# Seven block products in the down projections of a two-half-step SwiGLU layer, with the sums of x kept in DRAM

## The chip, the cores and the metric

The kernel runs on one core of a Trainium2 chip. The metric is the device time of one execution in microseconds (us), lower is better. TensorE (PE) multiplies, VectorE (DVE) and ScalarE (ACT) do elementwise work, GpSimd (POOL) issues accumulating DMAs and small things, SyncE (SP) issues the loads of the weights.

## The reference

One decoder layer on x of 256 rows and 2048 columns, all in float32:

```python
x = x + 0.5 * swiglu(rms_norm(x, ffn1_norm), ffn1_w_gate, ffn1_w_up, ffn1_w_down)
x = x + hybrid_mixer(rms_norm(x, mix_norm), ...)       # attention and gated linear attention
x = x + cross_attention(rms_norm(x, xattn_norm), rms_norm(mem, mem_norm), ...)
x = x + 0.5 * swiglu(rms_norm(x, ffn2_norm), ffn2_w_gate, ffn2_w_up, ffn2_w_down)

def swiglu(h, w_gate, w_up, w_down):
    return (jax.nn.silu(h @ w_gate) * (h @ w_up)) @ w_down
```

The hidden width D_FF is 5632. The change touches only the two SwiGLU half steps (`ffn1` and `ffn2`).

## The kernel before

**Precision.** Each float32 operand is a sum of two parts, high and low: ACT casts the high part (`wh`), DVE subtracts it to get the low part (`wl`). A product is three matmuls: high times high, high times low, low times high. `split` does this for a weight group of four K tiles by 512 columns (128 x 2048 elements, 1 MB); `wh` and `wl` have three buffers. The raw weights have six buffers in the half steps, loaded ahead by SP in the order of the program.

**A half step** (`ffn`). The hidden width is cut into 11 blocks of 512 columns, in three parts, `PARTS = ((0,1,2,3),(4,5,6,7),(8,9,10))`. For each block f of a part, gate and up are computed (K = 2048: four groups of K), then silu and the product, and `turn` transposes the result into `hT[f]`. At the end of a part the down projection adds the part's share to x: for each of four output chunks c of 512 columns, `proj` runs over the part's blocks (three or four groups of K), and the result goes into `xs[c]` on DVE. After the last part each finished chunk gets `after(c)`: the norm of the next stage (squares on ACT, transposes on PE), or in the second half step the store.

**Seven products.** For blocks 1 to 10, gate and up are computed as a pair: for the first two groups of K, the two row blocks of x (128 rows each), the two groups and the two matrices make a 2 x 2 by 2 x 2 block product, computed with seven products instead of eight (`head` and its inner `rest`). A product is 12 matmuls of 128 x 512. It needs sums of weight groups, made on DVE (`add`) and by accumulating DMAs on POOL (`accumulate`), and four sums of blocks of x, high and low (`sums`), made once in a half step by `sums_of` and kept in SBUF for the whole half step. `head` runs the first two products, whose results go to PSUM (`x`, `y`) and from there by ACT into `c0l` (`acc`) and `ys`; `rest` runs the others, subtracts on DVE (`c0r`, `c1r`), and then runs the plain groups (`mm3`, 24 matmuls a group). `ahead` calls the next pair's `head` before the last plain group. Block 0 is computed plainly, since the sums aren't there yet; while it runs, `load_x` brings x in, and ACT takes its squares for the norm r, which the activation needs.

**Order.** A scheduler orders the instructions of each engine by priority (`tc.high_priority`) and its own estimate of times; on the chip each engine works in that order.

Of the kernel before, what the change touches and what calls it, by code (L numbers as in the profile page):

```python
# [16 lines left out]
P = 128  # L17
# [30 lines left out]
def layer_kernel(ctx: ExitStack, tc: tile.TileContext, A: dict, out: bass.AP):  # L48
# [10 lines left out]


    phase = {}

    def open_phase(name, half_step):
        phase.update(half_step=half_step, loads=0,
# [8 lines left out]
    def FT(tag, bufs, shape, dt, name):  # L73
        return phase["pool"].tile(shape, dt, tag=tag, name=name, bufs=bufs)
# [61 lines left out]
    def split(wh, wl, src):  # L136
        SC.copy(wh, src)  # L137
        last_split[:] = [V.tensor_sub(wl, src, wh.bitcast(F32)).ins]  # L138
# [33 lines left out]

    def sums_of(ga, gb, put):
# [11 lines left out]
        for i, x in enumerate((sa, sb)):  # L187
            split(*put(i), x)

    def product(acc, lhs, w, start):  # L190

# [13 lines left out]
    def head(Wl, cl, Wr, cr, lhs, ab, sums):  # L205
# [5 lines left out]
        def parts(src):  # L211
            with tc.high_priority(WPRI):
                wh, wl = split_tiles(4, 512)
                split(wh, wl, src)
            return wh, wl
# [10 lines left out]
            return lambda k: lhs(4 * g + k, t)  # L226

        def s_(i):
            return lambda k: tuple(x[:, i, k] for x in sums)

        x, y = PM([P, 512], "x"), PM([P, 512], "y")
        c0l = pa.tile([P, 512], F32, tag="acc", name="acc")
# [7 lines left out]
            ys = W2([P, 512], "ys")  # L240
            SC.copy(ys, y)

        def rest(groups, ahead=None):
            c0r, c1r = (pa.tile([P, 512], F32, tag="acc", name="acc") for _ in range(2))
            add(ral, ral, rbr)
            product(x, s_(1), parts(ral), False)
            with tc.high_priority(WPRI):
                V.tensor_sub(c0r, ys, x)
            product(c0l, of(b, 0), parts(rbl), False)
            accumulate(ral, rbl)  # L250
            product(x, s_(2), parts(rar), False)
            with tc.high_priority(WPRI):
                V.tensor_sub(c1r, ys, x)
# [103 lines left out]
    def ffn(pre, r, after, fine=None, last=False):  # L357
# [14 lines left out]
            sl = slice(t * P, (t + 1) * P)  # L372
            return tuple(p[:, k % 4, sl] for p in hT[k // 4])

        sums = None
        heads = {}

        def begin(f):
            heads[f] = head(wg, f, wu, f, lhs_x, (0, 1), sums)

        for part in PARTS:
            for f in part:
                ahead = (lambda f=f: begin(f + 1)) if f + 1 in part else None
                if sums is None:
                    gate = proj(wg, f, lhs_x, range(4), fine)
                    if callable(r):
                        r = r()
                else:
                    gate, upv = heads.pop(f)((2, 3), ahead)
                sg = []  # L390
                with tc.high_priority(WPRI):
                    for t in range(TT):
                        s = W2([P, 512], "sg")
                        SC.activation(s, gate[t], AF.Silu, scale=r[:, t:t + 1])
                        sg.append(s)
                if sums is None:
                    sums = tuple(FT(n, 1, [P, 4, 4, P], F32R, n) for n in ("sh", "sl"))
                    with tc.issue_after(last_split[0]):
                        sums_of(xT[0], xT[1], lambda i: tuple(p[:, 2 * i:2 * i + 2] for p in sums))
                    upv = proj(wu, f, lhs_x, range(4), ahead=ahead)  # L400
                hs = []
                with tc.high_priority(WPRI):
# [3 lines left out]
                        hs.append(h)  # L406
                later(2, lambda f=f, hs=hs: turn(f, hs))
            end = part is PARTS[-1]
            for c in range(NC):
                ahead = (lambda: begin(part[-1] + 1)) if c == NC - 1 and not end else None  # L410
                acc = proj(wd, c, lhs_h, part, last=last and end and c == NC - 1, ahead=ahead)
                for t in range(TT):
                    V.scalar_tensor_tensor(xs[c][:, t], acc[t], 0.5, xs[c][:, t], op0=ALU.mult, op1=ALU.add)  # L413
                if end:
                    after(c)


    def head_scale(acc, r, r2, t, scale_in, sign, name):
# [627 lines left out]
```

## Time and profile before

| | |
|---|---|
| median of 3 runs | 1932.91 us (1932.5 to 1933.68) |
| profiled execution, its own time | 1933.82 us |
| its span | 1932.0 us |
| PE, DVE, ACT, POOL busy | 99%, 65%, 51%, 5% |
| HBM read | 370.72 MB |
| granted TensorE clock, mean | 0.997 |

The page of the profile gives the busy time of each engine, the chain of work that ended last, and groups of instructions by line, with the tile written, an arrow and the tiles read. Timeline rows give start, duration, engine, line, operation and, in brackets, how long the engine sat idle before and what released it. Rows by windows give, for a stretch, the busy time and number of instructions of each engine, the granted clock (PEclk, 1.00 is full), the busy share of the 16 DMA engines and their GB/s. Line 138 is the subtraction and line 137 the cast of a split, 165 to 167 the three matmuls of a plain group, 196 a product's matmul, 219 a sum of weights on DVE, 223 one by DMA, 235 and 241 the copies to `c0l` and `ys`, 248 and 253 the subtractions out of PSUM, 289 the low part of `hT`, 315 the squares, 394 the silu, 413 the addition into x, 468 the loads of x.

### The profile page before, as it was taken

What the parts mean: (1) busy time and instruction counts of PE and PEld (TensorE: products, weight loads), DVE (VectorE), ACT (ScalarE), POOL (GpSimd) and SP (SyncE); (2) the same over time, 40 slices, a digit from 0 to 9 for tenths busy, and PEclk for the clock granted to TensorE, in tenths of its full rate; (3) what the DMA queues carried; (4) which work ended last, traced back from release to release, by engine and by line L of the source; (5) the groups of instructions that cost most, each with busy time, mean ns of one, the idle gap of its engine ahead of it and who ended that gap; (6) DMA issues with size and microseconds to landing.
All of it is one profiled execution on the core that took longest, in us unless ns stands there. A gap on an engine that the chain in (4) does not pass through costs nothing.

```text
span 1932.0 us, 21279 instructions
## 1 busy us (share of the span) xinstructions
PE 1916.0 (99%) x8760; PEld 1589.1 (82%) x8760; DVE 1265.0 (65%) x956; ACT 981.6 (51%) x881; POOL 90.3 (5%) x95
## 2 busy tenths in 40 slices
PE   8999999999999999999999999999999999999999
PEld 6888888888888888778888889888888888888887
DVE  6786567774678555445776554878656777467853
ACT  6555345553456446444566445655534555445542
POOL 0000000000000000012221000000000000000000
PEclk8999999999999999999999999999999999999999
DMA  9677568775577634445456554577755777557861
GB/s 370 224 234 264 194 189 278 254 258 196 167 247 271 233 124 157 168 155 189 174 209 226 179 191 153 222 241 234 263 195 186 272 264 258 193 166 251 267 245 54
DMA packets 63293, 416.14 MB, mean 215 GB/s; under 512 B 7099, under 2 KB 8251, under 8 KB 14428
## 3 DMA queue, kind: packets, MB, share of 16 engines
q1 hardware_dynamic: 55996, 370.22, 51.2%
q0 software_dynamic: 5760, 41.95, 10.5%
q10 hardware_dynamic: 1440, 2.62, 0.4%
q8 instruction: 68, 1.11, 0.2%
q14 instruction: 29, 0.24, 0.0%
HBM read 370.72 MB, written 2.10 MB: 193 GB/s over the span
## 4 chain that ended last, share of the span: by engine, by line
PE 96%; DMA 1%; DVE 1%; ACT 1%; POOL 0%; issue 0%; SPq 0%; ACTq 0%; POOLq 0%
PE acc L166 22%; PE acc L167 22%; PE acc L165 22%; PE x L196 11%; PE acc L196 6%; PE y L196 3%; PE x L167 2%; PE x L165 2%; PE x L166 2%; DMA raw<-in_ffn_w_gate_dram 1%; PE tp L366 1%; DVE wl L138 0%; PE tp L326 0%; ACT wh L137 0%; POOL gsr L686 0%
## 5 line engine op out<-in xcount | busy, mean ns | idle before, releaser
L138 DVE TENSOR_TENSOR wl<-raw,wh 128x2048 fp32r<-128x2048 f32 (+2 forms) x410 | 920.4, 2259 | 537.8 <-ACT wh L137 536.4
L137 ACT CAST wh<-raw 128x2048 fp32r<-128x2048 f32 (+2 forms) x410 | 769.8, 1889 | 767.3 <-PE acc L167 467.0
L165 PE MATMUL acc<-wh,xTh 128*128 128x512 f32 x1024 | 402.5, 394 | 5.0 <-ACT wh L137 5.0
L166 PE MATMUL acc<-wl,xTh 128*128 128x512 f32 x1024 | 400.7, 391 | 3.6 <-DVE wl L138 3.6
L167 PE MATMUL acc<-wh,xTl 128*128 128x512 f32 x1024 | 400.4, 391 | 0.0
L165 PE MATMUL acc<-wh,hTh 128*128 128x512 f32 x704 | 274.7, 390 | 0.0
L167 PE MATMUL acc<-wh,hTl 128*128 128x512 f32 x704 | 274.0, 389 | 0.0
L166 PE MATMUL acc<-wl,hTh 128*128 128x512 f32 x704 | 273.9, 389 | 0.0
L165 PEld LDWEIGHTS acc<-wh,xTh 128*128 128x128 f32 x1024 | 192.6, 188 | 46.7 <-ACT wh L137 6.3
L166 PEld LDWEIGHTS acc<-wl,xTh 128*128 128x128 f32 x1024 | 193.4, 189 | 45.1 <-DVE wl L138 5.4
L167 PEld LDWEIGHTS acc<-wh,xTl 128*128 128x128 f32 x1024 | 193.2, 189 | 40.6
L167 PEld LDWEIGHTS acc<-wh,hTl 128*128 128x128 f32 x704 | 132.1, 188 | 27.4
L166 PEld LDWEIGHTS acc<-wl,hTh 128*128 128x128 f32 x704 | 132.2, 188 | 27.2
L165 PEld LDWEIGHTS acc<-wh,hTh 128*128 128x128 f32 x704 | 132.2, 188 | 27.2
L219 DVE TENSOR_TENSOR raw<-raw 128x2048 f32<-128x2048 f32 x40 | 91.7, 2292 | 1.4
L223 POOL DMA_DIRECT2D raw<-raw x40 | 34.7, 867 | 1142.5 <-DVE raw L219 939.3
L165 PE MATMUL x<-wh,xTh 128*128 128x512 f32 x160 | 62.2, 389 | 0.0
L166 PE MATMUL x<-wl,xTh 128*128 128x512 f32 x160 | 62.2, 389 | 0.0
L167 PE MATMUL x<-wh,xTl 128*128 128x512 f32 x160 | 62.2, 389 | 0.0
L413 DVE SCALAR_TENSOR_TENSOR x<-acc,x 128x512 f32<-128x512 f32 x48 | 33.0, 688 | 27.2 <-PE acc L167 27.2
L165 PE MATMUL acc<-wh,mTh 128*128 128x512 f32 x128 | 50.1, 392 | 0.0
L167 PE MATMUL acc<-wh,mTl 128*128 128x512 f32 x128 | 49.8, 389 | 0.0
(301 smaller groups left out, 1916.4 us busy)
## 6 DMA issues: line engine op xcount, KB each, us to landing
raw<-in_ffn_w_up_dram SPq DMA_DIRECT2D x88, 1024.0 KB, 6.7
raw<-in_ffn_w_down_dram SPq DMA_DIRECT2D x88, 1024.0 KB, 4.8
raw<-in_ffn_w_gate_dram SPq DMA_DIRECT2D x85, 1024.0 KB, 4.8
raw<-in_w_in_dram SPq DMA_DIRECT2D x48, 1024.0 KB, 4.8
raw<-raw POOLq DMA_DIRECT2D x40, 1024.0 KB, 7.1
raw<-in_w_out_dram SPq DMA_DIRECT2D x16, 1024.0 KB, 4.8
raw<-in_xattn_w_k_dram SPq DMA_DIRECT2D x4, 1024.0 KB, 4.8
raw<-in_xattn_w_q_dram SPq DMA_DIRECT2D x4, 1024.0 KB, 4.8
```

What stands on the lines that cost most here:

```text
L137: SC.copy(wh, src)
L138: last_split[:] = [V.tensor_sub(wl, src, wh.bitcast(F32)).ins]
L165: PE.matmul(acc[t], lh, wh, start=first and i == 0, stop=False, skip_group_check=seeded)
L166: PE.matmul(acc[t], lh, wl, start=False, stop=False, skip_group_check=seeded)
L167: PE.matmul(acc[t], ll, wh, start=False, stop=last and i == len(half) - 1, skip_group_check=seeded)
L196: PE.matmul(acc, lhs(k)[i], w[:, k], start=first, stop=j == 1 and k == 3, skip_group_check=not start)
L219: V.tensor_add(dst, x, y)
L223: G.dma_start(dst, x, accum_op=ALU.add)
L366: PE.transpose(tp[:, j], hs[t][:, j * P:(j + 1) * P], ident)
L413: V.scalar_tensor_tensor(xs[c][:, t], acc[t], 0.5, xs[c][:, t], op0=ALU.mult, op1=ALU.add)
```

## The change

The down projections use the seven products too: chunks are taken in pairs (0, 1) and (2, 3), as the left and right matrix of `head`, with the first two blocks of the part as the two groups of K. The other blocks of the part (two, or one in the last part) run as plain groups. This needs sums of blocks of `hT`, which `sums_of_halves` makes once a part, after the last product of the part's last block that uses sums of x (`mid`). The tiles of the sums are now four of one tag `s`, shared by x and h: the sums of x are written to DRAM once in a half step (`first_sums`), by DMAs of POOL, and are loaded back at the start of the second and third part (`load_sums`). In the last group of the second half step, `last` keeps the order of one row block after the other. The loads of x get lower priorities, one lower than the other. Block 0 stays plain.

```diff
+    dr = ctx.enter_context(tc.tile_pool(name="dr", bufs=1, space=bass.MemoryType.DRAM))
...
+    def S4(name):
+        return FT("s", 4, [P, 2, 4, P], F32R, name)
...
+    def sums_of_halves(ga, gb):
+        q = {}
+        for n, (h, l) in (("a", ga), ("b", gb)):
+            for t in (1, 0):
+                sl = slice(t * P, (t + 1) * P)
+                q[n, t] = W2([P, 4, P], "q")
+                V.tensor_add(q[n, t], h[:, :, sl].bitcast(F32), l[:, :, sl].bitcast(F32))
+        sums = [(S4("sh"), S4("sl")) for _ in range(2)]
+        def put(i, x):
+            h, l = sums[i // 2]
+            split(h[:, i % 2], l[:, i % 2], x)
+        V.tensor_sub(q["b", 1], q["a", 1], q["b", 1])
+        put(0, q["b", 1])
+        V.tensor_sub(q["a", 1], q["a", 0], q["a", 1])
+        V.tensor_sub(q["a", 0], q["b", 1], q["a", 0])
+        put(1, q["a", 0])
+        V.tensor_add(q["b", 0], q["b", 0], q["a", 0])
+        put(2, q["a", 1])
+        put(3, q["b", 0])
+        return sums
...
-        def rest(groups, ahead=None):
+        def rest(groups, ahead=None, mid=None, last=False):
...
             product(c0r, s_(3), parts(rbr), False)
+            if mid:
+                mid()
...
+                    if last and acc is accs[1] and i == len(groups) - 1:
+                        both = [w for half in wgroup(W, c, g) for w in half]
+                        for t in range(TT):
+                            mm3(acc, lhs, both, False, True, (t,), seeded=True)
+                        break
...
+        kept = [dr.tile([P, 2, 4, P], F32R, name=f"{pre}s{i}") for i in range(4)]
+        def first_sums():
+            sums["x"] = sums_of(xT[0], xT[1])
+            for i in range(4):
+                G.dma_start(kept[i], sums["x"][i // 2][i % 2])
+        def load_sums():
+            with tc.high_priority(WPRI):
+                sums["x"] = [tuple(S4(n) for n in ("sh", "sl")) for _ in range(2)]
+                for i in range(4):
+                    G.dma_start(sums["x"][i // 2][i % 2], kept[i])
...
+        def half_sums(part):
+            with tc.high_priority(WPRI // 2):
+                sums["h"] = sums_of_halves(hT[part[0]], hT[part[1]])
+        def begin_down(part, c):
+            heads["d", c] = head(wd, c, wd, c + 1, lhs_h, part[:2], sums["h"])
+        def next_part(part):
+            load_sums()
+            begin(part[-1] + 1)
...
-            for c in range(NC):
-                ahead = (lambda: begin(part[-1] + 1)) if c == NC - 1 and not end else None
-                acc = proj(wd, c, lhs_h, part, last=last and end and c == NC - 1, ahead=ahead)
-                for t in range(TT):
-                    V.scalar_tensor_tensor(xs[c][:, t], acc[t], 0.5, xs[c][:, t], op0=ALU.mult, op1=ALU.add)
-                if end:
-                    after(c)
+            for c in range(0, NC, 2):
+                ahead = (lambda: begin_down(part, c + 2)) if c == 0 else None if end else (lambda: next_part(part))
+                accs = heads.pop(("d", c))(part[2:], ahead, None, last and end and c > 0)
+                for d, acc in zip((c, c + 1), accs):
+                    for t in range(TT):
+                        V.scalar_tensor_tensor(xs[d][:, t], acc[t], 0.5, xs[d][:, t], op0=ALU.mult, op1=ALU.add)
+                    if end:
+                        after(d)
...
-            with tc.high_priority(WPRI):
+            with tc.high_priority(WPRI - 16 - 16 * c):
                 SY.dma_start(xs[c], A["x"][0, :, c * 512:(c + 1) * 512].rearrange("(t p) d -> p t d", p=P))
```

Line numbers of the changed kernel are others: the cast and the subtraction of a split are lines 139 and 140 there, a product's matmul 229, a sum of weights 252, the copies 268 and 274, the squares 355, the silu 458, the addition into x 477.

**On ACT, during block 0 of the first half step,** the last rows of the squares (`junk`) and what follows, before. `raw_347` is the first group of up's weights; `sh` are the high parts of the sums of x, `sg` is the silu:

```order
L315 ACTIVATE junk_315,ss1_298<-x3_106 128x512
L315 ACTIVATE junk_317,ss1_298<-x3_106 128x512
L137 CAST sh_329<-sa_335 128x1024
L137 CAST sh_329<-sb_336 128x1024
L394 ACTIVATE sg_325<-acc_128,r1_323 128x512
L394 ACTIVATE sg_327<-acc_129,r1_323 128x512
L137 CAST wh_349<-raw_347 128x2048
L137 CAST wh_379<-raw_377 128x2048
```

and in the changed kernel, where `raw_359` and `raw_389` are the first two groups of up:

```order
L139 CAST wh_262<-raw_260 128x1024 x2
L355 ACTIVATE junk_306,ss1_304<-x0_105 128x512
L355 ACTIVATE junk_308,ss1_304<-x0_105 128x512
L139 CAST wh_361<-raw_359 128x2048
L355 ACTIVATE junk_311,ss1_304<-x1_106 128x512
L355 ACTIVATE junk_313,ss1_304<-x1_106 128x512
L139 CAST wh_391<-raw_389 128x2048
L355 ACTIVATE junk_316,ss1_304<-x2_107 128x512
L355 ACTIVATE junk_318,ss1_304<-x2_107 128x512
L139 CAST sh_345<-sa_339 128x1024
L355 ACTIVATE junk_321,ss1_304<-x3_108 128x512
L355 ACTIVATE junk_323,ss1_304<-x3_108 128x512
```

The casts of up's first two groups now stand between the squares, ahead of the sums' casts and the silu, where before they came behind all of these.

**On ACT, where block 0 ends and the first pair with seven products begins,** before; `raw_437` is the left weight group of the pair, `raw_485` the last group of up of block 0:

```order
L137 CAST wh_409<-raw_407 128x2048
L137 CAST wh_448<-raw_437 128x2048
L137 CAST wh_467<-raw_437 128x2048
L137 CAST wh_487<-raw_485 128x2048
L137 CAST wh_522<-raw_437 128x2048
L235 COPY acc_447<-x_445 128x512
L137 CAST wh_539<-raw_443 128x2048
L241 COPY ys_483<-y_446 128x512
L137 CAST wh_572<-raw_439 128x2048
```

and in the changed kernel, from the silu on, where `raw_449` is that left group and `raw_497` the last group of up:

```order
L458 ACTIVATE sg_331<-acc_134,r1_329 128x512
L458 ACTIVATE sg_333<-acc_135,r1_329 128x512
L139 CAST wh_421<-raw_419 128x2048
L139 CAST wh_460<-raw_449 128x2048
L139 CAST wh_479<-raw_449 128x2048
L268 COPY acc_459<-x_457 128x512
L274 COPY ys_495<-y_458 128x512
L139 CAST wh_499<-raw_497 128x2048
L139 CAST wh_534<-raw_449 128x2048
```

Before, the cast of up's last group stood ahead of both copies out of PSUM; now it stands behind the copy to `ys`. On PE the order of groups stays, but three matmuls of the pair's third product now stand behind the first two of up's last group.

**On DVE, at the end of the first part,** behind the second subtraction out of PSUM of block 3, before (`hTl` is block 2's, then come splits of plain groups and of the first down group):

```order
L253 TENSOR_TENSOR acc_1076<-ys_1035,x_997 128x512
L289 TENSOR_TENSOR hTl_1112<-tp_1113,hTh_1111 128x4x128
L138 TENSOR_TENSOR wl_1192<-raw_989,wh_1191 128x2048
L289 TENSOR_TENSOR hTl_1112<-tp_1120,hTh_1111 128x4x128
L138 TENSOR_TENSOR wl_1210<-raw_1207,wh_1209 128x2048
L138 TENSOR_TENSOR wl_1240<-raw_1237,wh_1239 128x2048
L138 TENSOR_TENSOR wl_1270<-raw_1267,wh_1269 128x2048
L138 TENSOR_TENSOR wl_1310<-raw_1307,wh_1309 128x2048
L138 TENSOR_TENSOR wl_1356<-raw_1353,wh_1355 128x2048
```

and in the changed kernel, from the first difference of h's sums (`q`) on; `raw_1303` and `raw_1305` are the left and right weights of the first down pair:

```order
L213 TENSOR_TENSOR q_1177<-q_1173,q_1177 128x512
L329 TENSOR_TENSOR hTl_1124<-tp_1125,hTh_1123 128x4x128
L215 TENSOR_TENSOR q_1173<-q_1175,q_1173 128x512
L140 TENSOR_TENSOR sl_1182<-q_1177,sh_1181 128x512
L216 TENSOR_TENSOR q_1175<-q_1177,q_1175 128x512
L329 TENSOR_TENSOR hTl_1124<-tp_1132,hTh_1123 128x4x128
L140 TENSOR_TENSOR wl_1276<-raw_1273,wh_1275 128x2048
L140 TENSOR_TENSOR sl_1182<-q_1175,sh_1181 128x512
L140 TENSOR_TENSOR wl_1315<-raw_1303,wh_1314 128x2048
L218 TENSOR_TENSOR q_1179<-q_1179,q_1175 128x512
L252 TENSOR_TENSOR raw_1303<-raw_1303,raw_1305 128x2048
L140 TENSOR_TENSOR sl_1184<-q_1173,sh_1183 128x512
```

The sums of h and the subtractions of their low parts (`sl`) now stand between the splits of the part's last groups and the first sum of weights of the down pair; before, splits followed each other there.

More of the change, by code (lines that the diff above doesn't have):

```diff
@@ L186, in sums_of @@
         V.tensor_add(sb[:, 1], fb[:, :, t0], sa[:, 1])
-        for i, x in enumerate((sa, sb)):
-            split(*put(i), x)
+        sums = []
+        for x in (sa, sb):
+            h, l = S4("sh"), S4("sl")
+            split(h, l, x)
+            sums.append((h, l))
+        return sums
[18 more added lines that the diff above has]
+        put(3, q["b", 0])
+        return sums
     def product(acc, lhs, w, start):
@@ L228, in s_ @@
         def s_(i):
-            return lambda k: tuple(x[:, i, k] for x in sums)
+            return lambda k: tuple(x[:, i % 2, k] for x in sums[i // 2])
         x, y = PM([P, 512], "x"), PM([P, 512], "y")
@@ L388, in ffn @@
                 else:
-                    gate, upv = heads.pop(f)((2, 3), ahead)
+                    gate, upv = heads.pop(f)((2, 3), ahead, (lambda: half_sums(part)) if final else None)
                 sg = []
@@ L395, in ffn @@
                         sg.append(s)
-                if sums is None:
-                    sums = tuple(FT(n, 1, [P, 4, 4, P], F32R, n) for n in ("sh", "sl"))
+                if f == 0:
                     with tc.issue_after(last_split[0]):
-                        sums_of(xT[0], xT[1], lambda i: tuple(p[:, 2 * i:2 * i + 2] for p in sums))
+                        first_sums()
                     upv = proj(wu, f, lhs_x, range(4), ahead=ahead)
```

11 lines of the change are left out of this document (6 added, 5 removed).

## The prediction

> **What bounds the kernel now.** I read the page first: busy times, then the chain that ended last.
>
> ```profile
> PE 1916.0 (99%) x8760; PEld 1589.1 (82%) x8760; DVE 1265.0 (65%) x956; ACT 981.6 (51%) x881; POOL 90.3 (5%) x95
> PE 96%; DMA 1%; DVE 1%; ACT 1%; POOL 0%; issue 0%; SPq 0%; ACTq 0%; POOLq 0%
> ```
>
> PE (TensorE) is busy nearly always and 96% of the chain is PE. A busy PE need not be at its peak, so the second view is the timeline of PE, for the distance between starts (first column), in a product of seven (line 196):
>
> ```profile
> 150.63 1.07 PE L196 MATMUL x<-wh,sh 128*128 128x512 f32 x4
> 151.53 1.07 PE L196 MATMUL x<-wh,sl 128*128 128x512 f32 x4
> 152.44 1.07 PE L196 MATMUL x<-wl,sh 128*128 128x512 f32 x4
> 153.35 1.07 PE L196 MATMUL acc<-wh,xTh 128*128 128x512 f32 x4
> ```
>
> Twelve matmuls take 153.35 - 150.63 = 2.72 us, so one costs 0.227 us; the 0.39 us that the groups give as a mean overlaps its neighbours and is no price. A weight group of 24 costs 5.44 us. The third view sets stages side by side: a gate/up column block with products (67.23 to 109.00), down projections of the first part, and of the last.
>
> ```profile
> core 0: us, PE busy (x) PEld busy (x) DVE busy (x) ACT busy (x) POOL busy (x), PEclk, DMA share, GB/s
> 67.23:109.00 41.77, 41.77 (x190) 34.69 (x189) 33.15 (x19) 23.98 (x17) 1.73 (x2) 1.00 0.77 255
> 190.00:310.00 120.00, 120.00 (x535) 99.42 (x535) 72.57 (x42) 49.55 (x29) 2.59 (x3) 1.00 0.61 208
> 655.00:722.00 67.00, 67.00 (x314) 55.78 (x313) 40.70 (x34) 29.95 (x33) 0.62 (x3) 1.00 0.38 136
> ```
>
> PE has no idle time in any of them, at full clock. A stage with seven products loads DVE (VectorE) to 79% and the DMA engines to 77% and still runs at PE's pace; the down projections leave much more free. So matmuls taken out of the down projections shorten the span one for one, as long as DVE, ACT (ScalarE) and the loads keep up. The place where PE does wait is the start:
>
> ```profile
> 32.22 0.39 PE L167 MATMUL acc<-wh,xTl 128*128 128x512 f32 x1
> 35.70 0.88 PE L165 MATMUL acc<-wh,xTh 128*128 128x512 f32 x2 [3.09 <-ACT wh L137]
> 38.02 0.79 PE L166 MATMUL acc<-wl,xTh 128*128 128x512 f32 x1 [1.44 <-DVE wl L138]
> 42.88 0.43 PE L166 MATMUL acc<-wl,xTh 128*128 128x512 f32 x1
> 35.70:38.60 2.90, 1.46 (x3) 0.79 (x4) 2.90 (x2) 2.90 (x2) 0.00 (x0) 0.57 1.01 427
> 38.60:43.10 4.50, 4.50 (x12) 3.52 (x11) 3.77 (x2) 0.64 (x1) 0.00 (x0) 0.52 1.01 402
> ```
>
> Between gate and up of block 0 PE waits for the cast of up's first weights, then for their subtraction, and then 4.5 us run at a granted clock of 0.52. The matmul at 42.88 is the fourteenth of up; without a loss it would start at 32.45 + 13 x 0.227 = 35.40. So 7.5 us are lost there.
>
> **Term 1, the products.** Two groups of K, two output chunks and two row blocks make eight block products of 12 matmuls, now seven. A pair of chunks in a part saves 12 matmuls = 2.72 us. There are 2 pairs x 3 parts x 2 half steps = 12: 144 matmuls, 32.6 us, all of it on the path that sets the end.
>
> **Term 2, what the products add elsewhere.** The prices:
>
> ```profile
> L138 DVE TENSOR_TENSOR wl<-raw,wh 128x2048 fp32r<-128x2048 f32 x400 | 910.4, 2290 | 535.1 <-ACT wh L137 533.8
> L219 DVE TENSOR_TENSOR raw<-raw 128x2048 f32<-128x2048 f32 x40 | 91.7, 2292 | 1.4
> L413 DVE SCALAR_TENSOR_TENSOR x<-acc,x 128x512 f32<-128x512 f32 x48 | 33.0, 688 | 27.2 <-PE acc L167 27.2
> L253 DVE TENSOR_TENSOR acc<-ys,x 128x512 f32<-128x512 f32 x20 | 13.8, 689 | 0.0
> L137 ACT CAST wh<-raw 128x2048 fp32r<-128x2048 f32 x400 | 761.2, 1915 | 765.2 <-PE acc L167 467.0 <-PE x L167 128.5 <-DVE raw L219 103.5
> L241 ACT COPY ys<-y 128x512 f32<-128x512 f32 x20 | 11.6, 578 | 0.0
> ```
>
> Each pair adds three splits, two sums of weights and two subtractions out of PSUM: 3 x 2.28 + 2 x 2.29 + 2 x 0.69 = 12.8 us of DVE, 153 us over 12 pairs, on no path of their own in a part of four blocks: 180 matmuls (40.8 us) against 11 splits, 2 sums, 2 subtractions and 4 evictions, 11 x 2.28 + 4.6 + 1.4 + 2.8 = 33.8 us, 83%, close to the 79% that the block at 67.23 shows without a wait. I take 0; a loss begins only beyond 100%. ACT gets 3 x 1.9 + 2 x 0.58 = 6.9 us a pair and has more room than DVE.
>
> The last part has one plain group: 132 matmuls, 29.9 us, against 9 x 2.28 + 4.6 + 1.4 + 2.8 = 29.3 us of DVE, 98%. In the first half step the norm of chunks 0 and 1 now falls into the second pair (before it came one chunk at a time), 8 passes of 0.69 us = 5.5 us, so DVE would need about 5 us more than PE there, less what it is ahead (three buffers of split weights, up to 5.4 us of products). Bounds: 0 and about 5 us in the first half step, 0 and 1 in the second. I take 1.0 us together, near the lower end, since the stage at 67.23 stands nearest.
>
> **Term 3, the sums of h.** Once a part, 12 passes on DVE of 128x512 (0.69 us: 8.3 us) and four casts on ACT. By the order they stand between the last splits of the part's last block, where DVE idles 41.77 - 33.15 = 8.6 us. Two of the twelve come earlier, and only the first subtraction for the pair's second product is wanted within that stretch. What would be late next is the split for that product. Ends: 0 when covered and 6 x 8.3 = 50 us when nothing covers it; the row nearest is the 8.6 us, so 0.
>
> **Term 4, transfers.** Queue totals and the times of POOL's DMAs:
>
> ```profile
> q1 hardware_dynamic: 55996, 370.22, 51.2%
> q0 software_dynamic: 5760, 41.95, 10.5%
> DMA to landing us min/median/max: 6.8/7.1/9.0
> ```
>
> q0 holds the 40 accumulating DMAs: 0.105 x 1932 / 40 = 5.1 us of all engines each; a plain megabyte costs 0.512 x 1932 / 370.2 = 2.7 us. New are 24 accumulations, 122 us, and per half step 2.1 MB written once and read twice, 34 us together. The share goes from 62% to (1200 + 156) / 1900 = 71%. Per pair it is 8 x 2.8 + 10.2 = 32.6 us in 40.8 (80%; the block that runs freely has 77%), in the last part 6 x 2.8 + 10.2 = 27.0 in 29.9 (90%), in the pair after which the sums of x return 32.6 + 5.6 = 94%. That return is issued when the fourth of seven block products that use sums has been done; from there to PE's next need lie three groups and two products, 21.8 us, three times the median landing. On POOL nothing waits behind it: the next accumulation comes after the next block's first split. A transfer that is late by its whole time costs at most 5.6 us x 4 returns = 22 us. I take 0, as no row shows PE waiting for a load in a stage with products. The end of the kernel keeps its form (the last group runs one row block after the other, each followed by its eviction and store): 0.
>
> **Term 5, the start.** The loads of x now stand between those of up's weights, and ACT's order has up's casts between the squares. Before, the casts stood behind all squares, both sums' casts and the activation:
>
> ```profile
> 23.90 0.63 ACT L315 ACTIVATE junk<-x 128x512 f32<-128x512 f32 x1
> 32.59 1.27 ACT L394 ACTIVATE sg<-acc,r 128x512 f32<-128x512 f32 x2 [0.92 <-POOL r L342]
> 33.75 3.70 ACT L137 CAST wh<-raw 128x2048 fp32r<-128x2048 f32 x2
> raw<-in_ffn_w_up_dram SPq DMA_DIRECT2D x1, 1024.0 KB, 12.8
> L223 POOL DMA_DIRECT2D raw<-raw x40: 852/862/1045, 52.6 to 1820.7; - x40
> ```
>
> Up's first load was issued at 16.90 and landed 12.8 us later, at 29.7; with three x chunks behind it instead of ahead (1.5 MB at about 430 GB/s, 3.7 us) it lands near 26 and is cast by 28; by the order its subtraction stands behind four of the six passes that form the sums and ends near 31.3, ahead of 32.45. The 7.5 us go. On POOL the first store of the sums stands ahead of r, which the activation needs; its cast is done before the last squares, so it costs r at most its issue, 0.86 us, and the activation is not what PE waits for. But the order makes a new wait: the last group of up is cast only behind the copy of the second product's result (ys), which itself waits for PE to end that product. Then PE idles 0.1 + 0.58 + 1.91 = 2.6 us, runs two matmuls, and waits for one more cast, 1.9 - 0.45 = 1.45 us, since three matmuls of the next product stand ahead of the rest of the group. The clock: in the rows above two gaps of 3.09 and 1.44 us were followed by 0.52, which costs about ten matmuls 0.2 us each; smaller ones did it too:
>
> ```profile
> 13.56 0.73 PE L165 MATMUL acc<-wh,xTh 128*128 128x512 f32 x2 [1.11 <-ACT wh L137]
> 14.82 0.50 PE L166 MATMUL acc<-wl,xTh 128*128 128x512 f32 x1 [0.53 <-DVE wl L138]
> 15.60:19.00 3.40, 3.40 (x9) 2.60 (x8) 3.40 (x6) 3.33 (x6) 0.00 (x0) 0.51 1.05 436
> 1232.03 0.50 PE L166 MATMUL acc<-wl,xTh 128*128 128x512 f32 x1 [1.59 <-DVE wl L138]
> ```
>
> 1.11 and 0.53 us were enough at 13.56; one gap of 1.59 us at 1232 was followed by matmuls at full pace. Two gaps of together 4.05 us are nearest to the first two cases: I add 2.0 us. Start: 7.5 - 4.05 - 2.0 = 1.4 us gained. Bounds: 7.5 gained if the new wait doesn't come, 0 if it is a little longer.
>
> The Trainium skill, "TensorE: Matmul & The Clock Gate", under "What's actually happening", says the clock halves after an idle window of about 3.4 us, in a window that runs freely. Read strictly, gaps of 2.6 and 1.45 us with work between leave the clock up, and the start would gain 3.4 us, the sum 2.0 us less than mine; the rows at 13.56 speak against the strict reading, so the row decides, and that case is a rival below.
>
> **Sum.** -32.6 + 1.0 + 0 + 0 - 1.4 = -33.0 us. The profiled execution took 1933.82 us around a span of 1932.0; it lies 0.9 us above the median of 1932.91. So span 1899.0, profiled time 1900.8, median 1900.
>
> **Rivals.**
> - The clock stays up at the start, or the new wait there is shorter or missing: 1900 - 2 = 1898 to 1900 - 6 = 1894. For it: the gap at 1232 with no slow stretch. Against: the slow stretches after 13.56 and 35.70, and ys ahead of the cast.
> - A cover is thin: last part's DVE at its bound (4 us over my 1.0), or loads at 90 to 94% of the DMA engines make PE wait a few us at the four returns and the four pairs of the last parts (about 1 us each of 8). 1900 + 4 to 1900 + 12: 1904 to 1912. For it: 98% and 94%. Against: PE never waited at 79% and 77%.
> - DVE becomes the pace of the products (slower): seven splits, two sums, two subtractions are 21.9 us against 19.05 us of PE, and nothing of it is carried into the plain groups behind. 2.9 us x 12 = 34 us lost, more than term 1; with the sums of h uncovered 50 us more: 1900 + 84 = 1984. It decides against the change once over 2.7 us a pair is lost. Against: the block at 67.23 has the same products and DVE load, and PE does not wait.
> - The change doesn't do what it says: sums return too late in each part and eat the rest. Up to 22 us: 1922, still faster.
>
> **How the numbers follow.** My forecast 0.62 (own range 1897 to 1904), the start gaining more 0.14, thin covers 0.18, late sums 0.03, DVE's pace 0.03. The range 1894 to 1912 takes in the first three but for their tails, and leaves out about 1 in 10. About 0.2% (3.9 us) is what a measurement can tell from no change. Every case but DVE's pace is faster by more: faster 0.96; 0.01 for losses that happen to cancel 33 us; slower 0.03.
>
> **What would show it.** Right: 144 matmuls fewer, 36 splits and 24 weight sums more; 12 matmuls in 2.72 us in the down projections too; PE's waits for wh and wl outside the start under 2 us in sum; DVE near 77% of the span, the DMA engines near 71%; a gap of about 2.6 us near 54 us, with ACT's cast named as the releaser, in place of that at 35.70. Wrong: PE waiting for wl inside products of the down projections (DVE's pace), for sh or sl at a pair's second product (sums late), or the third gap of the start missing.

## The result, and the profile after

The changed kernel takes 1898.14 us (median of 4 runs, 1897.76 to 1898.49) against 1932.95 us of the kernel before beside it (1932.5 to 1933.68): 34.8 us less, a ratio of 0.982 with a 95% interval of 0.9803 to 0.9837. The forecast was 1900. The profiled execution took 1898.33 us around a span of 1896.3 us, 35.7 us less than the span before.

The page of the changed kernel, busy times, chain and the two large DMA queues:

```profile
PE 1882.5 (99%) x8616; PEld 1562.4 (82%) x8616; DVE 1449.8 (76%) x1112; ACT 1070.9 (56%) x965; POOL 122.7 (6%) x143
PE 95%; DMA 1%; DVE 1%; ACT 1%; issue 1%; POOL 0%; SPq 0%; ACTq 0%; DVEq 0%
q1 hardware_dynamic: 55996, 370.22, 51.1%
q0 software_dynamic: 12672, 79.70, 19.1%
```

8760 - 8616 = 144 matmuls are gone. DVE went from 65% to 76% and the two queues from 62% to 70%, and PE is still the chain. The same by windows: two whole pairs of chunks in part 1, the two of the last part, and the stretch around the change of parts in which the sums of x come back:

```profile
202.83:243.63 40.80, 40.80 (x181) 33.80 (x180) 33.05 (x21) 21.76 (x13) 3.88 (x6) 1.00 0.81 261
243.63:284.43 40.80, 40.80 (x181) 33.79 (x180) 32.76 (x20) 21.76 (x13) 1.75 (x2) 1.00 0.89 304
633.91:664.77 30.86, 30.86 (x142) 25.54 (x141) 27.20 (x18) 20.17 (x16) 1.72 (x2) 1.00 0.77 258
664.77:694.70 29.93, 29.93 (x141) 24.88 (x140) 28.46 (x21) 21.15 (x23) 0.86 (x1) 1.00 0.70 196
236.00:262.00 26.00, 26.00 (x117) 21.53 (x116) 19.89 (x12) 11.84 (x7) 1.93 (x3) 1.00 1.04 380
```

A pair takes 40.80 us for 180 matmuls, 0.227 each, with no idle time of PE, DVE at 81% (33.05 of 40.80) and at 95% in the last part (28.46 of 29.93). The last row is the tightest place: for 26 us the DMA engines are full. The start, on PE and on ACT:

```profile
51.65 1.07 PE L229 MATMUL y<-wl,sh 128*128 128x512 f32 x4
55.19 0.98 PE L167 MATMUL acc<-wh,xTh 128*128 128x512 f32 x2 [2.47 <-ACT wh L139]
56.99 1.65 PE L229 MATMUL x<-wh,sh 128*128 128x512 f32 x3 [0.82 <-ACT wh L139]
58.44 0.63 PE L168 MATMUL acc<-wl,xTh 128*128 128x512 f32 x1
58.86 0.63 PE L169 MATMUL acc<-wh,xTl 128*128 128x512 f32 x1
...
62.53 0.39 PE L167 MATMUL acc<-wh,xTh 128*128 128x512 f32 x1
...
52.75 0.58 ACT L274 COPY ys<-y 128x512 f32<-128x512 f32 x1 [2.10 <-PE y L229]
53.23 5.50 ACT L139 CAST wh<-raw 128x2048 fp32r<-128x2048 f32 x3
```

The stall at 35.70 is gone. ACT waits for PE to end the second product, copies it to `ys`, and only then casts the last group of up: PE sits idle for 2.47 and 0.82 us and then runs at 0.43 us a matmul until about 62.3.

To set kernels side by side I add up, over the matmuls of 512 columns, what each distance between two starts exceeds 0.227 us. This is PE's lost time:

| kernel | span | start to 20 us | 20 to 80 us | rest of half step 1 | mixer, attention | half step 2 | sum |
|---|---|---|---|---|---|---|---|
| before | 1932.0 | 4.2 | 7.6 | 1.5 | 5.6 | 1.0 | 19.8 |
| after | 1896.3 | 1.9 | 6.7 | 1.7 | 5.4 | 1.0 | 16.7 |

32.6 us of matmuls and 3.1 us of lost time make up the 35.7 us. The down projections lost nothing.

### The profile page after: what moved, and what is told of

It reads as the page before. It is cut to its first block, busy times and chain, and to the rows that moved or that the text cites. A ratio compares the mean times of both kernels' runs of the same rounds, so it can differ in the third digit from the quotient of the medians.

```text
span 1896.3 us, 21437 instructions
## 1 busy us (share of the span) xinstructions
PE 1882.5 (99%) x8616; PEld 1562.4 (82%) x8616; DVE 1449.8 (76%) x1112; ACT 1070.9 (56%) x965; POOL 122.7 (6%) x143
## 4 chain that ended last, share of the span: by engine, by line
PE 95%; DMA 1%; DVE 1%; ACT 1%; issue 1%; POOL 0%; SPq 0%; ACTq 0%; DVEq 0%
PE x L229 18%; PE acc L168 17%; PE acc L169 17%; PE acc L167 17%; PE acc L229 9%; PE y L229 4%; PE x L168 3%; PE x L167 3%; PE x L169 3%; DMA raw<-in_ffn_w_gate_dram 1%; PE tp L406 1%; ACT wh L139 1%; DVE wl L140 1%; PE tp L366 0%; POOL gsr L750 0%
## 5 line engine op out<-in xcount | busy, mean ns | idle before, releaser
L140 DVE TENSOR_TENSOR wl<-raw,wh 128x2048 fp32r<-128x2048 f32 (+2 forms) x446 | 999.0, 2260 | 325.8 <-ACT wh L139 324.2
L139 ACT CAST wh<-raw 128x2048 fp32r<-128x2048 f32 (+2 forms) x446 | 836.2, 1891 | 643.0 <-PE acc L169 205.3
L252 DVE TENSOR_TENSOR raw<-raw 128x2048 f32<-128x2048 f32 x64 | 146.6, 2290 | 1.7
L169 PE MATMUL acc<-wh,hTl 128*128 128x512 f32 x240 | 93.4, 389 | 0.0
L167 PE MATMUL acc<-wh,hTh 128*128 128x512 f32 x240 | 93.4, 389 | 0.0
L168 PE MATMUL acc<-wl,hTh 128*128 128x512 f32 x240 | 93.4, 389 | 0.0
L229 PE MATMUL x<-wh,sh 128*128 128x512 f32 x256 | 71.5, 401 | 0.8 <-ACT wh L139 0.8
L229 PE MATMUL x<-wh,sl 128*128 128x512 f32 x256 | 68.5, 390 | 0.0
L229 PE MATMUL x<-wl,sh 128*128 128x512 f32 x256 | 68.5, 390 | 0.0
L168 PE MATMUL x<-wl,xTh 128*128 128x512 f32 x160 | 62.3, 389 | 0.0
L167 PE MATMUL x<-wh,xTh 128*128 128x512 f32 x160 | 62.3, 389 | 0.0
L169 PE MATMUL x<-wh,xTl 128*128 128x512 f32 x160 | 62.3, 389 | 0.0
L229 PEld LDWEIGHTS x<-wh,sl 128*128 128x128 f32 x256 | 48.1, 188 | 10.2
```

The source lines that it names most:

```text
L167: PE.matmul(acc[t], lh, wh, start=first and i == 0, stop=False, skip_group_check=seeded)
L168: PE.matmul(acc[t], lh, wl, start=False, stop=False, skip_group_check=seeded)
L169: PE.matmul(acc[t], ll, wh, start=False, stop=last and i == len(half) - 1, skip_group_check=seeded)
L229: PE.matmul(acc, lhs(k)[i], w[:, k], start=first, stop=j == 1 and k == 3, skip_group_check=not start)
L252: V.tensor_add(dst, x, y)
```

## The experiments

Theory A is the prediction's: the span is the count of matmuls at 0.227 us, plus the gaps that PE shows, and nothing of what the products add elsewhere is on the path. The main rivals are B (much of the gain comes from the start or the loads) and C (the covers are thin). Every time stands beside runs of the kernel before on the same chip (1933.4 to 1933.6 us). Lost time of all kernels, summed as above:

| kernel | time us | ratio to before, interval | 0-20 | 20-80 | rest 1 | middle | half step 2 |
|---|---|---|---|---|---|---|---|
| after_again | 1898.78 | 0.9819 (0.9805 to 0.9832) | 2.0 | 6.7 | 1.7 | 5.4 | 1.0 |
| loads_only | 1929.97 | 0.9984 (0.9975 to 0.9993) | 1.9 | 7.2 | 1.5 | 5.6 | 1.0 |
| old_loads | 1900.36 | 0.9831 (0.9817 to 0.9844) | 2.1 | 9.0 | 1.6 | 5.5 | 1.0 |
| dead12 | 1931.34 | 0.9991 (0.9982 to 1.0) | 2.1 | 8.0 | 1.4 | 5.6 | 1.2 |
| dma2 | 1898.49 | 0.9818 (0.9805 to 0.9832) | 2.3 | 6.9 | 2.4 | 5.4 | 1.0 |
| dve1_all | 1917.45 | 0.9911 (0.9897 to 0.9924) | 2.1 | 7.3 | 13.7 | 5.6 | 7.2 |
| dve3_mid | 1912.56 | 0.9897 (0.9882 to 0.9912) | 2.0 | 7.7 | 7.2 | 5.5 | 7.0 |
| dve3_last | 1921.53 | 0.9941 (0.9928 to 0.9953) | 2.0 | 6.6 | 13.0 | 5.6 | 12.0 |
| ys_late2 | 1896.52 | 0.9812 (0.9799 to 0.9825) | 2.0 | 4.8 | 1.7 | 5.4 | 2.2 |
| stores_late | 1897.84 | 0.9819 (0.9806 to 0.9833) | 2.5 | 5.9 | 1.7 | 5.4 | 1.0 |
| best1 | 1901.26 | 0.9839 (0.9826 to 0.9853) | 2.3 | 2.6 | 3.1 | 5.4 | 6.2 |
| best2 | 1892.4 | 0.9787 (0.9774 to 0.9801) | 2.1 | 0.7 | 1.8 | 5.3 | 1.0 |

**The changed kernel again.** 

> The changed kernel once more, beside the others of this call: 0.982 of the time before, 1898 to 1899.

It came out as expected and is what the others are compared with: two executions lose the same in every stage, within 0.1 us. From 20 to 80 us they do so in other places: this one lost 1.1 us near 42 us and some 5.5 at the wait near 55 us, the first one 6.6 there.

**The two parts of the change, apart.** `loads_only` is the kernel before with

```diff
-            with tc.high_priority(WPRI):
+            with tc.high_priority(WPRI - 16 - 16 * c):
                 SY.dma_start(xs[c], ...)
```

and `old_loads` is the changed kernel with that line put back.

> The kernel before with the new priorities of the loads of x alone; no product is added. Theory A (the span is the count of matmuls at 0.227 us plus the gaps that PE shows): only the start moves. The stall between gate and up of block 0 goes (7.6 us by the changed kernel's trace), the wait behind the copy of ys comes (6.6 us with its slow stretch), so 1.0 us gained, 2.7 us if the calmer gate stage comes from the loads too: 1930 to 1932. Theory B (much of the 35 us comes from the start or the order of the loads, and a product is worth less than its matmuls): 1925 or less.

> The changed kernel with the old priorities of the loads of x. Theory A: the stall between gate and up comes back (+7.6 us); by the order of ACT a cast now stands ahead of the copy of ys, so the wait near 55 us goes (-6.6 us): 1899 to 1901, within 3 us of the changed kernel. Theory B: 1905 or more.

`loads_only` gained 3.6 us (1.4 to 4.8), a little more than expected; `old_loads` lies about 2 us above the changed kernel, as expected, though the two intervals overlap. So the products with the old loads are worth 33.2 us (1933.55 - 1900.36), and B fails. What the loads alone are worth is less clear. By the stages `loads_only` lost 0.4 us less than the kernel before between 20 and 80 us; the other 2.3 us lie in the first 20 us, where `old_loads`, without the new loads, lost as little. In both traces the start exchanges one stall for another; first row `old_loads`, second `loads_only`:

```profile
35.33 1.16 PE L167 MATMUL acc<-wh,xTh 128*128 128x512 f32 x2 [4.68 <-ACT wh L139]
```

```profile
56.91 0.79 PE L196 MATMUL x<-wh,sh 128*128 128x512 f32 x1 [2.66 <-ACT wh L137]
```

**The matmuls put back.** `dead12` runs one product more a pair in the down projections:

```diff
-            product(c0r, s_(3), parts(rbr), False)
+            wd4 = parts(rbr)
+            product(c0r, s_(3), wd4, False)
+            if Wl is Wr:
+                product(y, s_(3), wd4, True)
```

> The changed kernel with one product more (12 matmuls) in each pair of chunks of the down projections, into a PSUM bank that nobody reads, from a weight group that is split anyway: the 144 matmuls are back and everything else of the change stays. Theory A: +144 x 0.2267 = 32.6 us, 1930.8, give or take 0.7. Theory C (DVE, ACT or the transfers already set the pace in some of the pairs, and the products hide there): less, by what those covers cost; under 1926.

1931.34 us, 32.6 more than the changed kernel again, as theory A has it; C asked for less than 1926. The splits, sums of weights, accumulating transfers and returns of the sums are all still there. The nearest kernel without them is `loads_only`, with the same number of matmuls and the same loads: `dead12` lies 1.4 us above it by the medians, 0.8 us of it between 20 and 80 us. So together they cost about 1 us (1.1 by the sums of lost time), and the 144 matmuls are the gain.

**How thick the covers are.** Passes of DVE more, in pairs of parts 1 and 2 (`dve3_mid`), in the last parts (`dve3_last`), or one in each pair (`dve1_all`):

```diff
             product(c0r, s_(3), parts(rbr), False)
+            if Wl is Wr and ...:
+                with tc.high_priority(WPRI):
+                    for _ in range(3):
+                        V.tensor_add(rbr, rbr, rbr)
```

> The changed kernel with three passes of DVE more, of 2.29 us each, in each pair of chunks in parts 1 and 2 (8 pairs), on a weight group whose use is over. DVE then has 33.05 + 6.9 = 39.9 us of work in the 40.80 us of a pair, 98%. Theory A (a loss begins only beyond 100%): 1 us or less slower than the changed kernel, so about 0.982 of the time before. Theory C (the cover is thin, PE waits for subtractions well before DVE is full): the passes stand in PE's way, up to 8 x 6.9 = 55 us, 1.01 of the time before; a part of it if only some are in the way.

> The same three passes in the pairs of the last parts alone (4 pairs). DVE then needs 34.1 us against 30.86 of PE, 35.3 against 29.93, and in the second half step 34.1 against 30.83 and 32.7 against 29.89: 14.6 us more than PE in sum. Theory A: a loss of 4 to 15 us, since split weights of up to 5.4 us per half step are ready ahead: 1902 to 1913. Theory C': DVE carries far more ahead than three buffers: under 2 us.

> The changed kernel with one pass of DVE more (2.29 us) in each of the 12 pairs of chunks. DVE then fills 87% of a pair in parts 1 and 2, and 96, 103, 95 and 94% of the four pairs of the last parts. Theory F (DVE's share decides, with a loss that begins between 90 and 98%): 0 in parts 1 and 2, 1 to 3 us in the last parts: 1899 to 1902. Theory G (in an ordered queue each pass delays what stands behind it, at any share; three passes cost 1.8 us a pair): 12 x 0.6 = 7 us: 1905.

All three cost more than was expected: 14, 23 and 19 us. With one pass in each pair, 13.3 us of the lost time lie at the changes of parts behind the pairs of parts 1 and 2 (PE's stops near 271, 524, 1473 and 1724 us) and 4.9 us in the last parts; three passes in parts 1 and 2 lose 11.5 us, in those pairs and in the blocks behind them (near 228, 289 and 311 us and in the same places of the other parts). So it is not the number of passes, or DVE's share, that pays. The trace of `dve1_all` names what does; SP's load, ACT and DVE at the change from part 1 to 2:

```profile
241.35 3.13 SPq L133 DMA_DIRECT2D raw<-in_ffn_w_gate_dram  x2
254.77 1.91 ACT L139 CAST wh<-raw 128x2048 fp32r<-128x2048 f32 x1 [4.46 <-DMA raw<-in_ffn_w_gate_dram]
236.24 0.69 DVE L281 TENSOR_TENSOR acc<-ys,x 128x512 f32<-128x512 f32 x1
236.84 4.49 DVE L140 TENSOR_TENSOR wl<-raw,wh 128x2048 fp32r<-128x2048 f32 x2
241.84 2.28 DVE L291 TENSOR_TENSOR raw<-raw 128x2048 f32<-128x2048 f32 x1
259.05 2.29 DVE L252 TENSOR_TENSOR raw<-raw 128x2048 f32<-128x2048 f32 x1
270.74 0.54 PE L168 MATMUL acc<-wl,hTh 128*128 128x512 f32 x1 [3.11 <-DVE wl L140]
```

The same rows of the changed kernel, of SP, ACT and DVE:

```profile
238.66 2.53 SPq L133 DMA_DIRECT2D raw<-in_ffn_w_gate_dram  x2
247.91 3.73 ACT L139 CAST wh<-raw 128x2048 fp32r<-128x2048 f32 x2 [4.43 <-PE x L169]
235.75 0.69 DVE L281 TENSOR_TENSOR acc<-ys,x 128x512 f32<-128x512 f32 x1
236.34 4.48 DVE L140 TENSOR_TENSOR wl<-raw,wh 128x2048 fp32r<-128x2048 f32 x2
254.38 2.29 DVE L252 TENSOR_TENSOR raw<-raw 128x2048 f32<-128x2048 f32 x1
```

And one row of the waits (us in total, times, longest), of `dve1_all` and then of the changed kernel:

```profile
ACT wh L139 <- DMA raw<-in_ffn_w_gate_dram: 17.1, 6, 4.5
```

```profile
ACT wh L139 <- DMA raw<-in_ffn_w_gate_dram: 2.3, 2, 1.4
```

Line 291 is the extra pass. In the changed kernel gate's first load goes out as soon as the first of the two splits at 236.34 has ended (238.62). In `dve1_all` the split in that place ends at 239.13 and no load follows: the load goes out behind the second split (241.33), and gate's second one, at 244.15, behind the extra pass (241.84 + 2.28 = 244.12). So the extra pass keeps a raw weight buffer some 5 us longer, 2.28 us of its own and the rest for its place in DVE's order; which buffer each load takes is not in the rows, it is read from these times. The first load is issued 2.7 us later, into the stretch where the DMA engines are full. ACT waits 4.46 us for it, where the changed kernel casts that group without a wait (the row at 247.91 holds two casts). The sum of weights on DVE starts 4.67 us later, and PE waits 3.11 us. Since the program stood 0.49 us later there anyway, the changed kernel has 4.67 - 0.49 - 3.11 = 1.1 us in reserve at that place. `dve3_mid` shows the same wait of ACT for gate's loads, 17.0 us. In `dve3_last` it is DVE's order, as theory G has it: the passes stand ahead of the low part of `hT` and of a split that PE needs next, as PE's timeline shows:

```profile
663.50 1.21 PE L229 MATMUL x<-wl,hTh 128*128 128x512 f32 x4 [3.76 <-DVE wl L140]
668.51 0.80 PE L169 MATMUL acc<-wh,hTl 128*128 128x512 f32 x1 [3.79 <-DVE hTl L333]
```

F and G both missed the size, and at the changes of parts the mechanism was neither. How much of `dve3_mid` is DVE's own queue and how much the held buffer was not separated, since every pass here also held a buffer.

**More transfers.** `dma2` copies the raw group `rbl` to DRAM twice in each pair of parts 1 and 2:

```diff
+                    for i in range(2):
+                        spare = dr.tile([P, 4, 512], F32, name=...)
+                        G.dma_start(spare, rbl)
```

> The changed kernel with two transfers more of 1 MB each, from a raw weight group to DRAM, on POOL's queue, in each pair of chunks of parts 1 and 2 (16 MB). By 2.7 us of all engines for a megabyte the DMA engines go from 81 to 94% in a part's first pair and from 89 to 102% in its second. Theory A (transfers hide until their engines are full): 4 us or less, 1898 to 1902. Theory H (POOL's order or the raw buffer that each transfer holds longer makes a load late): 5 us or more, with PE waiting for casts that wait for loads.

No loss: 1898.49 us, 0.3 us below the changed kernel again. But POOL did not issue the copies behind the products, where the program has them: each went out as soon as `rbl` had landed, one pair's at 166.03 us, still in block 3, and the other's at 208.19, in the first pair. The queue on the page, that row of POOL, the two pairs of part 1 by windows, and two shorter stretches:

```profile
q0 software_dynamic: 14976, 96.48, 21.1%
208.19 1.10 POOL L295 DMA_DIRECT2D spare<-raw  x2 [20.17 <-DMA raw<-in_ffn_w_down_dram]
```

```profile
202.83:243.63 40.80, 40.80 (x182) 33.79 (x181) 33.07 (x21) 21.77 (x14) 4.98 (x8) 1.00 0.93 315
243.63:284.43 40.80, 40.80 (x182) 33.80 (x181) 32.77 (x20) 21.76 (x14) 1.77 (x3) 1.00 0.89 305
210.00:220.00 10.00, 10.00 (x46) 8.26 (x44) 7.91 (x4) 3.15 (x2) 0.87 (x1) 1.00 1.02 397
236.00:262.00 26.00, 26.00 (x117) 21.52 (x116) 19.89 (x13) 11.45 (x7) 1.93 (x3) 1.00 1.03 381
```

From 210 to 220 us the DMA engines are full (0.63 in the changed kernel) and PE does not wait. The 16.8 MB more on this queue cost 2.0% of the span, 38 us, or 2.3 us a megabyte. So full DMA engines alone cost nothing there. The second pair stayed at 0.89, though, and the crowded stretch from 236 to 262 us got none of the copies (1.03 against 1.04). Nor did a buffer come free later: gate's load is issued at 239.05, 0.39 us after that of the changed kernel, as far as the program stands later there. So this run does not test the tightest place, and theory H stays open. With `dve1_all` it points to the moment at which a raw buffer comes free before the crowded stretch, and not to the share of the transfers; no run here has a fuller crowded stretch without a held buffer.

**The wait at the start.** `ys_late2` moves, for the first pair of blocks in each half step, the copy to `ys` from `head` into `rest`, and holds the next sum of weights behind the last group's subtraction:

```diff
-            SC.copy(ys, y)
+            if not late:
+                SC.copy(ys, y)
...
+            if late:
+                SC.copy(ys, y)
...
+                with tc.issue_after(last_split[0]):
+                    add(ral, ral, rbr)
```

> The changed kernel with two steps of the first pair (blocks 1) moved in order: the copy of the second product's result to ys behind the casts, and the next sum of weights behind the subtraction for the last group of up. Theory A: the wait of 2.5 us near 55 us, the second of 0.8 to 1.4 us and the slow stretch behind them go together, 6.6 us: 1891.5; 1893 to 1896 if one gap of about 2 us is left there. Theory D (the slow stretch near 57 to 62 us has a cause of its own, and the gaps only happen to stand ahead of it): only the gaps' 3.9 us, 1894, with a stretch at a granted clock near 0.5 still in the trace.

1896.52 us, some 2 us better instead of 6.6; its four runs lie between 1895.03 and 1898.83, and its interval overlaps that of the changed kernel. The profile lost 1.9 us less between 20 and 80 us, but 1.2 us more in the second half step. The wait moved on; PE, then ACT, of `ys_late2`:

```profile
53.39 0.73 PE L167 MATMUL acc<-wh,xTh 128*128 128x512 f32 x2 [0.59 <-ACT wh L139]
55.71 0.79 PE L168 MATMUL acc<-wl,xTh 128*128 128x512 f32 x1 [1.59 <-DVE wl L140]
56.30 0.63 PE L169 MATMUL acc<-wh,xTl 128*128 128x512 f32 x1
51.43 1.91 ACT L139 CAST wh<-raw 128x2048 fp32r<-128x2048 f32 x1 [0.69 <-DMA raw<-in_ffn_w_up_dram]
```

Behind the copy the load of the last group was late too. The stores of the sums, 2.1 MB, run in the same stretch. `stores_late` queues them on POOL behind the first two accumulating transfers (`issue_after`), `best1` does that on top of `ys_late2`:

> The changed kernel with the four stores of the sums of x (2.1 MB in each half step) queued on POOL behind the two accumulating transfers of the first pair, instead of ahead of them. Theory A: in the changed kernel the wait near 55 us ends with the copy of ys, and no load, so the stores cost nothing there: within 1 us of it. Theory E (the loads set the pace of the whole start, at 420 GB/s, and the stores take 2.1 MB = 4.9 us of them): up to 4.9 us faster.

> The kernel with the first pair's copy and sum moved behind the last group of up (the run with 1896.5), and the stores of the sums queued late as well. There the last group's load was the last to come, 2.1 MB behind time. Theory E: it now comes 3.7 to 4.9 us sooner, the gaps of 0.6 and 1.6 us near 54 us and the slow stretch behind them go, 4.6 us in sum: 1892. Theory A': something else is as late as that load (the subtraction on DVE): a gap of 1 us or more stays, 1894 to 1896.

`stores_late` changed nothing, as theory A had it: with the copy in the way the load doesn't matter. `best1` got worse, 1901.26 us. From 20 to 80 us it loses 2.6 us only, but the stores now take the place of loads for block 2, most in the second half step, and at the start another copy (to `c0l`) stood ahead of the cast:

```profile
50.08 0.57 ACT L268 COPY acc<-x 128x512 f32<-128x512 f32 x1 [4.01 <-PE x L229]
54.85 0.50 PE L168 MATMUL acc<-wl,xTh 128*128 128x512 f32 x1 [1.60 <-DVE wl L140]
1278.18 1.91 ACT L139 CAST wh<-raw 128x2048 fp32r<-128x2048 f32 x1 [5.23 <-DMA raw<-in_ffn_w_gate_dram]
```

`best2` takes all three into account: both copies are issued behind the cast, in the first half step only, and the stores behind block 2's accumulating transfers.

> The changed kernel with the first pair of the first half step in another order: both copies out of PSUM behind the cast of up's last group, the next sum of weights behind its subtraction, and the stores of the sums of x behind block 2's accumulating transfers instead of the first or block 1's. Theory A: all three that were late in turn (copy, load, copy again) are now in time, so 5 to 6.6 us faster than the changed kernel, 1892 to 1893, with no gap over 0.6 us between 45 and 110 us. Theory I (one late thing is only followed by the next): a gap of 1.5 us or more with its slow stretch stays there, 1895 or more.

1892.4 us (1891.99 to 1893.07), 6.4 us below the changed kernel again, whose runs lie between 1897.33 and 1899.32: the best version here, 41 us below the kernel before. Its page has PE at 97% of the chain, and in the timeline PE goes through the place without a stop:

```profile
PE 97%; DVE 1%; DMA 1%; ACT 0%; POOL 0%; issue 0%; SPq 0%; ACTq 0%
```

```profile
51.52 1.07 PE L229 MATMUL y<-wl,sh 128*128 128x512 f32 x4
52.43 0.62 PE L167 MATMUL acc<-wh,xTh 128*128 128x512 f32 x2
...
57.87 1.07 PE L229 MATMUL x<-wh,sh 128*128 128x512 f32 x4
```

From 52.43 to 57.87 are 5.44 us, 24 matmuls at full pace. So the gap and the half clock behind it went together (theory D fails), and three things had been late one behind the other: copy, load, copy. Each step took some 2 us out of the stage from 20 to 80 us (6.7, 4.8, 2.6 and 0.7 us lost), but the first two lost time elsewhere. A run with both copies moved and the stores left in place is missing.

## Why the prediction was right, step by step

- **Term 1, the products: -32.6 us, right.** 144 matmuls fewer at 0.227 us; `dead12` gave 32.6 us back.
- **Term 2, DVE and ACT: +1.0 us, measured about 0** (no stop of PE in a down projection; `dead12` lies 1.4 us above `loads_only`, none of it in the down projections of the first half step). The step "in the last part DVE would need about 5 us more than PE" was mis-sized: 98% was forecast for a plain pair, and 5.5 us more for the one with the norm; that one measured 95% (28.46 us in its window). Its sentence "a loss begins only beyond 100%" is wrong as a rule: `dve1_all` lost 13.3 us behind pairs where DVE had 87%, because a raw buffer came free later.
- **Term 3, the sums of h: 0, right.** No stop of PE in any down projection.
- **Term 4, transfers: 0, right, for a weaker reason than given.** A share of 94% was forecast for the pair with the return and 89% measured, but the 26 us around the change of parts are full (1.04), and the reserve of the loads there is about 1.1 us. The rival of thin covers did not happen and was nearer than its chance of 0.18 sounds.
- **Term 5, the start: -1.4 us, measured -3.2 in the two profiles.** The stall between gate and up (7.5 us) went, as forecast. The new wait came at its place with its releaser, and cost 6.6 us (some 5.5 when the kernel ran again) instead of 6.05: in the profile idle 2.47 and 0.82 us by the rows, 2.6 and 1.2 us by the distances between starts, and some twelve matmuls instead of ten at half clock. So the stage from 20 to 80 us gained 0.9 us (7.6 - 6.7), a little less than forecast. The other 2.3 us lie in a stage that the forecast took as unchanged: up to 20 us the profile before lost 4.2 us, the one after 1.9. `old_loads`, whose engines work in the same order as before up to there, lost 2.1, and the other kernels 1.9 to 2.5. The profile before has a longer wait at 13.56 (1.11 us) and a slow stretch behind it. Not every execution seems to have that stretch: of the 21 runs of the kernel before beside `loads_only`, the 13 with a mean granted clock of 0.997, as in the profile, have a median of 1933.6 us, and the 8 with 0.998 one of 1932.4. So a part of these 2.3 us belongs to the execution and not to the change; why the wait at 13.56 was longer stays open.

The medians moved by 34.8 us, 1.8 us more than the 33.0 of the sum: 1.0 us of term 2 did not come, 0.5 us less than forecast came from 20 to 80 us, and some 1.3 us come from elsewhere, by the profiles from the first 20 us. No term of the sum stands for these, so that the total lies so close is in part luck. The rival that the clock stays up did not happen. By the window of about 3.4 us in the Trainium skill, "TensorE: Matmul & The Clock Gate", under "What's actually happening", read strictly, it should have; the trace does not agree with that reading, since idle times of 3.11 us alone (`dve1_all`, at 270.74, the next matmuls 0.43 us apart) and of 0.59 and 1.59 us close together (`ys_late2`) were followed by half clock. The length agrees: the slow stretches last 3.41 us or a multiple of it (last section).

## What to carry to other kernels

- Where PE is gap-free in the trace, matmuls taken out pay one for one, and putting dead ones back is the cheapest proof of it.
- A busy share below 100% is no proof of a cover: what counts is the reserve at the tightest place, here the moment a buffer is released ahead of a stretch with full DMA engines. A pass that costs the engine nothing can still hold a buffer.
- When one wait is removed, look for what is late behind it before building: here a copy hid a load, and the load another copy. Moving the first, or the first two, paid 2 us or nothing; moving all three paid 6.4 us.

## What the runs showed of the hardware

The traces hold the granted clock with its times. Between the first 7 and the last 2 us of a span it is 1.00 or 0.50, and each slow stretch of the 14 traces lasts 3.41 us or two or three times as long; within an execution the changes lie on a grid of 3.41 us. Windows of this grid in the changed kernel, around the wait near 55 us:

```profile
52.08:55.49 3.41, 0.94 (x4) 0.48 (x3) 1.43 (x2) 2.74 (x3) 0.00 (x0) 1.00 1.05 249
55.49:62.32 6.83, 6.01 (x15) 4.19 (x14) 6.37 (x3) 3.24 (x2) 0.86 (x1) 0.50 0.85 244
62.32:65.73 3.41, 3.41 (x17) 2.80 (x15) 1.01 (x2) 0.26 (x1) 0.00 (x0) 1.00 1.04 216
```

In the window that ends at 55.49 PE is idle for 3.41 - 0.94 = 2.47 us, and the next two run at half clock. With all 14 traces cut into these windows, half clock followed 21 windows at full clock, with 1.64 to 3.41 us of idle time, and none with 1.60 us or less; one window with 1.91 us (`dve3_last`, at 658.24) was followed by full clock. A slow stretch went on behind a window with 0.65 us of idle time or more, and ended behind one with 0.49 or less. So in these runs idle time adds up within such a window, and the step lies a little above 1.6 us. Single gaps of 1.59 us, as at 1232 in the kernel before, stayed below it; 1.11 and 0.53 us in one window (12.23 to 15.64 there) did not. A gap that a window's edge divides counts in two windows, so one and the same wait can be followed by one slow window or by two: by two in the changed kernel, by one when it ran again (57.53 to 60.94 us). That wait cost 6.6 and some 5.5 us.

An accumulating transfer of 1 MB costs the DMA engines about twice a plain one: 5.1 us in the kernel before against 2.3 us for the copies to DRAM in `dma2` and 2.7 us for the loads of the kernel before.
